# Turning attention probabilities with VectorE and DMA instead of TensorE, with four engine queues in program order

## The chip, the core and the metric

The kernel runs on one core of a Trainium2 chip. The metric is the device time of one execution in microseconds (us). The core's engines are TensorE (PE: matmuls, with its weight loads listed apart as PEld), VectorE (DVE), ScalarE (ACT), GpSimd (POOL) and SyncE (SP, which here only issues DMAs). Each runs its own queue of instructions in order and waits on semaphores for the others.

## What is computed

Two layers over one sequence of 512 tokens of width 1024, in float32: a state-space mixer (layer 0) and a latent attention (layer 1), each behind an RMS norm and added to the residual, then a last RMS norm. The change lies in layer 1:

```python
def mla_mixer(u, positions, in_w, q_norm_w, kv_norm_w, uq_w, ukv_w, out_w):
    proj = u @ in_w                                    # c_q 384, c_kv 256, k_r 64, z 2048
    q = (rms_norm(c_q, q_norm_w) @ uq_w)               # 16 heads of 128 + 64 (rope)
    kv = (rms_norm(c_kv, kv_norm_w) @ ukv_w)           # 16 heads of 128 (keys) + 128 (values)
    ...
    o = causal_block_attention(q_full, k_full, v, MLA_QK_DIM ** -0.5)
    o = o.reshape(bsz, seq, MLA_WIDTH) * jax.nn.silu(z)
    return o @ out_w

# causal_block_attention, for each block of 128 queries:
    s = jnp.where(key_pos[None, :] <= q_pos[:, None], s, -jnp.inf)
    p = jax.nn.softmax(s, axis=-1)
    return jnp.einsum('bhqk,bkhd->bqhd', p.astype(v.dtype), v)
```

## The kernel before

Every float32 matrix product is made of three passes of fp32r matmuls: each operand is split into a high part (a cast, by ACT) and the rest (a subtraction, by DVE), and high x high, high x rest and rest x high are summed in PSUM. So each weight and each activation costs ACT a cast and DVE a subtraction. Weights come as units of 512 KB or less from DRAM into a raw tile (2 buffers, `load_weight`, L260), and `split_weight` (L266) makes whi and wlo (3 buffers each). `prefetch` (L252) loads and splits ahead of use in the order of the list `self.wq`: it splits one weight ahead (`LOOK = 1`) and loads one further.

PE's instructions stand in program order (`tc.manual_schedule` for PE). The other engines' order is chosen by the tile framework's scheduler. `sched` (L237) interleaves two things on PE: a feed, a generator that yields after every few matmuls with their cost, and pieces, functions that each have a due time on the feed's clock.

Layer 1 (`mla`, L650) first projects the input, writes the turned residual to DRAM (ht to hd: VectorE's 32x32 transposes and DMAs with runs of 128 B, L680 to L685), and then goes over 16 heads. For head h the feed is `front_a` in even heads (one rope product for two heads, then q and k of the next pair's first head, L725), `front_b` in odd heads (q and k of the second head, then both heads' values, L750), up to head 10 one gate product `zgemm` (L706), and from head 11 on steps of the first half of the output projection (`out_tok`, L908; KO steps per head). The pieces are:

- `score(h + 1, b)` (L783), b = 0 to 3, due at SC: the next head's scores for query block b, over n = 128 (b + 1) keys: five matmul passes (three for b = 0), mask and row minimum on DVE (L805), exponential with its sum on ACT (L223), reciprocal and scaling on DVE (L807, L808). The probabilities p are queries x keys.
- `turn(h, kb)` (L813), due at TU: for key block kb, PE transposes the 128x128 blocks of p into a PSUM bank (L817, ten per head), ACT casts them to ph (L821), DVE subtracts to get pl (L822).
- `product(h, kb)` (L825), due at PR: three matmuls with the values va, vb into the bank po; after the last one DVE multiplies by the gate z (L837).

`zsilu` (L715) puts SiLU on four gates at a time at the start of heads 4, 8 and 12; the table of functions that ACT holds changes for it, and back for the next exponential. `rope` (L692) multiplies by cosines and, after four swapping DMAs, by sines: three DVE operations. All DMAs of the attention (weights, swaps, residual) are issued by SP. PSUM has eight banks, which scores, products, turned blocks and fronts share in rotation.

Of the kernel before, what the change touches and what calls it, by code (L numbers as in the profile page):

```python
# [15 lines left out]
P = 128  # L16
# [34 lines left out]
OA = 8  # L51
SQ = 2

# [98 lines left out]
class Net:  # L152
# [8 lines left out]
    def build(self):  # L161
# [18 lines left out]
        self.phase, self.group, self.before, self.head = "", [], [], None  # L180
        self.wq = []
        self.wpos = self.wload = 0
        self.wraws = []
        self.wready = {}
        for g in range(NG):
            for i in range(6):
                self.wq.append(("w", U_IN + 6 * g + i))
# [6 lines left out]
        for h in range(14):  # L194
            j = h // 2 + 1
            self.wq += [("ua", j)] if h % 2 == 0 else [("ub", j), ("uc", j)]
            if h < 11:
                self.wq.append(("w", U_MZ + 5 + h))
            self.wq += [out.pop(0) for _ in range({11: 1, 12: 1, 13: 2}.get(h, 0))]
# [6 lines left out]
        with tc.tile_pool(name="ps_m", bufs=1, space=bass.MemoryType.PSUM, reuse_waits="tile") as ps, \  # L206
                tc.tile_pool(name="mla", bufs=2, reuse_waits="tile") as wk:
            self.ps, self.wk = ps, wk
            self.mla()

    LOOK = 1

    def link(self, ins, others):
        for o in others:
# [3 lines left out]
    def E(self, out, in_, func, **k):  # L218
        if self.phase != "E":
            pre = self.nc.scalar.preload_act_table_set("natural_log_exp_and_others")  # L220
            self.link(pre, self.group)
            self.phase, self.group, self.head = "E", [pre], pre
        i = self.nc.scalar.activation(out, in_, func, **k)  # L223
# [23 lines left out]
    def weight(self, kind, idx):  # L247
        key = (kind, idx)
        self.prefetch(self.wq.index(key) + 1 + self.LOOK)
        return self.wready.pop(key)  # L250

    def prefetch(self, want):  # L252
        while self.wload < min(want + 1, len(self.wq)):
            self.wraws.append(self.load_weight(*self.wq[self.wload]))
            self.wload += 1
        while self.wpos < min(want, len(self.wq)):
            self.wready[self.wq[self.wpos]] = list(self.split_weight(self.wraws.pop(0)))[-1]
            self.wpos += 1

    def load_weight(self, kind, idx):  # L260
        n = {"w": 1024, "ua": 1024, "ub": 640, "uc": 512}[kind]
        raw = self.wraw.tile([P, n], F32, tag="raw", name=self.nm("raw"))
        self.nc.sync.dma_start(raw[:], self.t[kind][idx])
        return raw

    def split_weight(self, raw, cuts=()):  # L266
# [4 lines left out]
        for a, b in zip((0, *cuts), (*cuts, n)):  # L271
            nc.scalar.copy(hi[:, a:b], raw[:, a:b])  # L272
            nc.vector.tensor_tensor(lo[:, a:b], raw[:, a:b], hi[:, a:b].bitcast(F32), op=ALU.subtract)  # L273
# [29 lines left out]
    def run(self, g):  # L303
        for _ in g:
            pass
# [54 lines left out]
    def ssm(self):  # L360
# [45 lines left out]
        for i, w in enumerate(ws):  # L406
            self.wready[self.wq[i]] = next(w)
# [242 lines left out]
    def mla(self):  # L650
        tc, nc, t, wk = self.tc, self.nc, self.t, self.wk
        v = nc.vector
        self.bufs = {"b": 8}
        col = lambda i: self.cols[:, i:i + 1]
# [16 lines left out]
        for i in range(6):  # L671
# [6 lines left out]
            if i >= 2:  # L678
                for k in (2 * i - 4, 2 * i - 3):
                    ht = wk.tile([P, T], F32, tag=("ph", "pl")[k % 2], name=self.nm("ht"))  # L680
# [11 lines left out]
        def rope(raw):  # L692
            sw = wk.tile([P, T], F32, tag="rsw", name=self.nm("rsw"), bufs=1)
            for i in range(4):
                j = i ^ 1
                nc.sync.dma_start(sw[32 * i:32 * i + 32, :], raw[32 * j:32 * j + 32, :])
# [374 lines left out]
```

## Time and profile before

| | |
|---|---|
| Median of 3 runs | 836.78 us (836.75 to 837.99) |
| Profiled execution | 836.13 us, of it span 834.0 us |
| Mean granted clock of TensorE | 0.999 |
| ACT busy | 450.4 us (54%) |
| DMA, mean over the span | 109 GB/s, 90.55 MB |
| DMA packets | 50,856, of them 21,552 under 512 B |

The span goes from the first to the last instruction of one profiled execution; the rest of its time lies around the span. A busy time is the part of the span in which the engine had an instruction under way. Matmuls overlap, so the time of one is best read from the starts of its neighbours. A group row ends with the idle time of the engine just before the group's instructions and with what ended it.

### The profile page before, as it was taken

The page shows a single profiled execution, that of the slowest core. Times are in us where ns is not written, and L with a number is a line of the kernel's source. Part 1 is how long each engine was busy: PE and PEld are TensorE (multiplying, and loading weights), DVE is VectorE, ACT ScalarE, POOL GpSimd, SP SyncE. Part 2 cuts the span into 40 slices and gives each one's busy share as a digit, 9 for nine tenths or more (in the row PEclk, how much of TensorE's full clock was granted, in tenths as well). Part 3 has the DMA queues.
Part 4 walks back from the last instruction along what each step waited for, and adds up shares of the span by engine and source line. Part 5 has one row for each costly group of instructions (what it writes and reads, how often), then busy time and mean ns, then how long its engine had stood idle before and what let it go on. Part 6 is the DMA issues. An engine that isn't in the chain of part 4 may idle for free.

```text
span 834.0 us, 11549 instructions
## 1 busy us (share of the span) xinstructions
PE 819.3 (98%) x4228; PEld 691.8 (83%) x4228; DVE 644.9 (77%) x1234; ACT 450.4 (54%) x794; POOL 0.2 (0%) x4
## 2 busy tenths in 40 slices
PE   7999999999999999999999999999999999999996
PEld 5887888888888888888888888888888888888885
DVE  7999898979787989778566787786767869675544
ACT  7567755545465657434353654556547557554233
POOL 0000000000000000000000000000000000000000
PEclk9999999999999999999999999999999999999999
DMA  6364543423242423333555142222222224331212
GB/s 227 103 191 141 155 147 106 152 99 129 101 139 90 152 76 127 115 121 94 130 130 132 54 130 64 79 72 76 63 64 58 90 78 152 101 97 56 86 66 101
DMA packets 50856, 90.55 MB, mean 109 GB/s; under 512 B 21552, under 2 KB 23088, under 8 KB 50800
## 3 DMA queue, kind: packets, MB, share of 16 engines
q1 hardware_dynamic: 50080, 88.77, 34.0%
q10 hardware_dynamic: 720, 1.05, 0.3%
q8 instruction: 33, 0.54, 0.3%
q14 instruction: 23, 0.19, 0.1%
HBM read 83.12 MB, written 4.33 MB: 105 GB/s over the span
## 4 chain that ended last, share of the span: by engine, by line
PE 92%; DVE 3%; DMA 2%; ACT 1%; SPq 1%; issue 0%; DVEq 0%; ACTq 0%
PE mm L291 55%; PE ot L941 11%; PE s L793 5%; PE mm L300 4%; PE po L835 4%; PE mm L773 3%; PE pt L817 2%; PE yd L138 2%; PE yd L291 1%; PE aux L130 1%; PE aux L105 1%; DMA x<-in_x_dram 1%; PE aux L77 1%; PE aux L89 1%; DMA L<-ac_d 1%; DVE wlo L273 1%
## 5 line engine op out<-in xcount | busy, mean ns | idle before, releaser
L272 ACT CAST whi<-raw 128x1024 fp32r<-128x1024 f32 (+3 forms) x132 | 127.0, 965 | 210.3 <-PE mm L291 172.8
L273 DVE TENSOR_TENSOR wlo<-raw,whi 128x1024 fp32r<-128x1024 f32 (+3 forms) x132 | 146.8, 1115 | 54.6 <-ACT whi L272 54.3
L291 PE MATMUL mm<-ah,whi 128*128 128x512 f32 x384 | 154.0, 401 | 0.0
L291 PE MATMUL mm<-ah,wlo 128*128 128x512 f32 x384 | 150.3, 391 | 0.4 <-DVE wlo L273 0.4
L291 PE MATMUL mm<-al,whi 128*128 128x512 f32 x384 | 149.9, 390 | 0.0
L291 PE MATMUL mm<-vh,whi 128*128 128x512 f32 x224 | 89.4, 399 | 0.8 <-ACT whi L272 0.8
L291 PE MATMUL mm<-vh,wlo 128*128 128x512 f32 x224 | 87.9, 392 | 0.7 <-DVE wlo L273 0.7
L291 PE MATMUL mm<-vl,whi 128*128 128x512 f32 x224 | 87.6, 391 | 0.0
L291 PEld LDWEIGHTS mm<-ah,wlo 128*128 128x128 f32 x384 | 72.1, 188 | 16.1 <-DVE wlo L273 0.8
L291 PEld LDWEIGHTS mm<-ah,whi 128*128 128x128 f32 x384 | 72.2, 188 | 15.3 <-issue 1.4
L291 PEld LDWEIGHTS mm<-al,whi 128*128 128x128 f32 x384 | 72.2, 188 | 14.4 <-DVE al L312 0.3
L941 PE MATMUL ot<-whi,ah 128*128 128x512 f32 (+1 forms) x136 | 52.4, 385 | 0.0
L941 PE MATMUL ot<-whi,al 128*128 128x512 f32 (+1 forms) x136 | 51.5, 379 | 0.0
L941 PE MATMUL ot<-wlo,ah 128*128 128x512 f32 (+1 forms) x136 | 51.4, 378 | 0.0
L291 PEld LDWEIGHTS mm<-vh,wlo 128*128 128x128 f32 x224 | 42.1, 188 | 10.7 <-DVE wlo L273 1.5
L291 PEld LDWEIGHTS mm<-vh,whi 128*128 128x128 f32 x224 | 42.2, 188 | 9.4 <-ACT whi L272 1.1
L223 ACT ACTIVATE p<-p,st 128x128 f32<-128x128 f32 (+1 forms) x64 | 36.1, 564 | 25.3 <-DVE st L805 25.2
L291 PEld LDWEIGHTS mm<-vl,whi 128*128 128x128 f32 x224 | 42.2, 188 | 7.3
L821 ACT CAST ph<-pt 128x512 fp32r<-128x512 f32 (+1 forms) x64 | 26.4, 421 | 33.3 <-PE pt L817 32.8
L291 PE MATMUL mm<-ch,whi 128*128 128x512 f32 x104 | 42.6, 410 | 0.0
L291 PE MATMUL mm<-ch,wlo 128*128 128x512 f32 x104 | 40.9, 393 | 0.0
L291 PE MATMUL mm<-cl,whi 128*128 128x512 f32 x104 | 40.8, 392 | 0.0
(223 smaller groups left out, 1637.7 us busy)
## 6 DMA issues: line engine op xcount, KB each, us to landing
raw<-in_w_dram SPq DMA_DIRECT2D x100, 512.0 KB, 3.3
L<-ac_d SPq DMA_DIRECT2D x32, 256.0 KB, 3.9
E<-ea_d SPq DMA_DIRECT2D x32, 128.0 KB, 3.5
raw<-in_ua_dram SPq DMA_DIRECT2D x8, 512.0 KB, 3.3
raw<-in_ub_dram SPq DMA_DIRECT2D x8, 320.0 KB, 2.8
x<-in_x_dram SPq DMA_DIRECT2D x8, 256.0 KB, 4.4
res<-in_x_dram SPq DMA_DIRECT2D x8, 256.0 KB, 3.1
hd<-ht SPq DMA_DIRECT2D x32, 64.0 KB, 3.5
```

The costliest lines, as they stand in the source:

```text
L138: nc.tensor.matmul(yd[64 * h:64 * h + 64, s], self.xdt[j][:, c, h, :], self.L[2 * j + h][:, s], start=True, stop=True)
L223: i = self.nc.scalar.activation(out, in_, func, **k)
L272: nc.scalar.copy(hi[:, a:b], raw[:, a:b])
L273: nc.vector.tensor_tensor(lo[:, a:b], raw[:, a:b], hi[:, a:b].bitcast(F32), op=ALU.subtract)
L291: self.nc.tensor.matmul(ps, a, b, start=i == 0, stop=i == len(seq) - 1)
L300: self.nc.tensor.matmul(p, seq[i][0], seq[i][1], start=i == 0, stop=i == 3 * ks - 1)
L773: nc.tensor.matmul(ps[:, c2 * 256:(c2 + 1) * 256], a, b, start=i == 0, stop=i == 5)
L793: nc.tensor.matmul(ps[:, :n], x[:, s], y[:, :n], start=k == 0, stop=k == 4)
L817: nc.tensor.transpose(pt[:, (b - kb) * P:(b - kb + 1) * P], probs[h][b][:, kb * P:(kb + 1) * P], self.ident)
L821: nc.scalar.copy(ph[:, :n], pt[:, :n])
L835: nc.tensor.matmul(po[:, kb * P:], x, y, start=kb == 0 and k == 0, stop=kb == NCH - 1 and k == 2)
L941: nc.tensor.matmul(ps[:, a:b], x, y, start=start and i == 0, stop=stop and i == 5)
```

## The change

1. **No transposes on PE.** `score` gets a `finish`: after the reciprocal and the scaling DVE turns the block in 32x32 squares (`v.transpose` into pb, 2 buffers), and SP writes it in four DMAs, in runs of 128 B, into a DRAM matrix pd (two, for even and odd heads), keys x queries. `fetch(h)`, a fifth piece of a head's scores, reads the four key blocks back (pl, in buffers of their own for even and odd heads). `turn` is only the cast pl to ph on ACT and the subtraction pl - ph on DVE, in place.
2. **Four queues in program order.** SP's instructions stand in program order in all of `mla`; in the loop over heads DVE, ACT and POOL do too. Subtractions, exponentials, `finish`, the rope and its casts are put off with `defer`: one to five yields of the feed later, or when their result is needed (`now`, `settle`). Without the loop's `lagging` flag they run at once, as before.
3. **Weights and swaps on POOL's queue** in `mla`, and weights split two ahead in the loop (`look = 2`).
4. **New places**: SF, SC, TU, PR and KO. In the heads the first two splits (0.08, 0.17) lie among the next head's scores (0.0 to 0.28), the others (0.47, 0.57) behind the first two products (0.35, 0.45). Head 0's scores move from beside `zgemm(4)` to beside `front_b(0)`. The values' products are a generator of their own, `front_v`, behind the gate product of odd heads. The silus move to 0.8 of heads 3, 7 and 11, with the table change behind them. The output projection splits two gates ahead (`OA = 2`, before 8), and reads the residual at its third weight.

The core of the diff:

```diff
-SF = (0.02, 0.1, 2.1, 3.1)
-SC = (0.0, 0.16, 0.25, 0.44)
-TU = (0.02, 0.08, 0.38, 0.55)
-PR = (0.3, 0.48, 0.65, 0.94)
-KO = (3, 4, 5, 8, 10)
+SF = (0.6, 1.0, 2.0, 3.2, 8.0)
+SC = (0.0, 0.1, 0.18, 0.28, 0.55)
+TU = (0.08, 0.17, 0.47, 0.57)
+PR = (0.35, 0.45, 0.74, 0.94)
+ZS = 0.8
+KO = (4, 4, 4, 8, 10)
-OA = 8
+OA = 2
...
+    def defer(self, fn, lag=1):
+        e = Later(fn, lag)
+        if self.lagging:
+            self.later.append(e)
+        else:
+            e.now()
+        return e
+
+    def tick(self):
+        for e in list(self.later):
+            e.lag -= 1
+            if e.lag <= 0:
+                e.now()
+        self.later = [e for e in self.later if not e.done]
...
         for cost in feed:
             done += cost
+            self.tick()
             while pieces and pieces[0][0] <= done:
                 pieces.pop(0)[1]()
...
-        self.nc.sync.dma_start(raw[:], self.t[kind][idx])
+        self.wqueue.dma_start(raw[:], self.t[kind][idx])
...
+        self.wqueue = nc.gpsimd
...
+            er = self.defer(functools.partial(rope, raw, sw), 3)
+            ea = self.defer(casts, 4)
+            f["w"].append(self.defer(rests, 5))
             yield 1.3
...
-            self.E(p[:], p[:], AF.Exp, scale=-1.0, bias=st[:, 0:1], accum_out=st[:, 1:2])
-            v.reciprocal(st[:, 2:3], st[:, 1:2])
-            v.tensor_scalar(p[:], p[:], st[:, 2:3], None, op0=ALU.mult)
-            probs[h].append(p)
+            p_exp = self.defer(functools.partial(
+                self.E, p[:], p[:], AF.Exp, scale=-1.0, bias=st[:, 0:1], accum_out=st[:, 1:2]))
+
+            def finish():
+                p_exp.now()
+                v.reciprocal(st[:, 2:3], st[:, 1:2])
+                v.tensor_scalar(p[:], p[:], st[:, 2:3], None, op0=ALU.mult)
+                pb = wk.tile([P, T], F32, tag="pb", name=self.nm("pb"))
+                v.transpose(pb[:, :n], p[:])
+                turned = pd[h % 2][:].rearrange("(j a) q -> a j q", a=32)
+                for i in range(4):
+                    q = b * P + 32 * i
+                    nc.sync.dma_start(turned[:, :n // 32, q:q + 32],
+                                      pb[32 * i:32 * i + 32, :n].rearrange("a (j q) -> a j q", q=32))
+
+            ends.append(self.defer(finish, 2))
...
+        def fetch(h):
+            while ends:
+                ends.pop(0).now()
+            for kb in range(NCH):
+                n = T - kb * P
...
+                nc.sync.dma_start(pl.bitcast(F32), pd[h % 2][kb * P:(kb + 1) * P, kb * P:])
+                back[h, kb] = pl
...
         def turn(h, kb):
             n = T - kb * P
-            pt = self.bank("pt")
-            for b in range(kb, NCH):
-                nc.tensor.transpose(pt[:, (b - kb) * P:(b - kb + 1) * P], probs[h][b][:, kb * P:(kb + 1) * P],
-                                    self.ident)
+            pl = back[h, kb]
             ph = wk.tile([P, T], F32R, tag="ph", name=self.nm("ph"))
-            pl = wk.tile([P, T], F32R, tag="pl", name=self.nm("pl"))
-            nc.scalar.copy(ph[:, :n], pt[:, :n])
-            v.tensor_tensor(pl[:, :n], pt[:, :n], ph[:, :n].bitcast(F32), op=ALU.subtract)
-            parts[h].append((ph, pl))
+            nc.scalar.copy(ph[:, :n], pl.bitcast(F32))
+            e = self.defer(functools.partial(
+                v.tensor_tensor, pl, pl.bitcast(F32), ph[:, :n].bitcast(F32), op=ALU.subtract))
+            parts[h].append((ph, pl, e))
...
+        with self.tc.manual_schedule(engines={E.SP, E.DVE, E.Activation, E.Pool}):
+            self.lagging, self.look = True, 2
+            self.sched(chain(front_b(0), front_v(0), zgemm(4)), list(zip(SF, steps(0))))
+            for h in range(MH):
...
+                if h % 2 and h < 14:
+                    feed.append(front_v(j))
                 at = SC if h + 1 < MH else ()
-            pieces = [(x * cost, functools.partial(score, h + 1, b)) for b, x in enumerate(at)]
+                pieces = [(x * cost, fn) for x, fn in zip(at, steps(h + 1))]
...
+                if h < 13 and h % 4 == 3:
+                    pieces.append((ZS * cost, functools.partial(zsilu, h // 4 + 1)))
```

More of the change, by code (lines that the diff above doesn't have):

```diff
@@ L184, in build @@
         self.wready = {}
+        self.later, self.wlater, self.cuts = [], [], {}
         for g in range(NG):
@@ L195, in build @@
             j = h // 2 + 1
[L196 to L199, printed above, removed]
+            self.wq.append(("ub" if h % 2 else "ua", j))
+            self.wq.append(("w", U_MZ + 5 + h) if h < 11 else out.pop(0))
+            if h % 2:
+                self.wq.append(("uc", j))
         self.wq += out
@@ L304, in run @@
         for _ in g:
-            pass
+            self.tick()
     def split(self, src, tagp, pool, n=T, tag=None):
@@ L703, in mla, with settle @@
         zt = []
-        F = [{} for _ in range(8)]
+        F = [{"w": []} for _ in range(8)]
+        def settle(f):
+            for e in f["w"]:
+                e.now()
+            f["w"] = []
         def zgemm(i):
@@ L861, in norm, with steps @@
             return hs, ls
+        def steps(h):
+            return [functools.partial(score, h, b) for b in range(NCH)] + [functools.partial(fetch, h)]
         outg = out0()
```

204 lines of the change are left out of this document (131 added, 73 removed).

## The prediction

> **What bounds the kernel now.** I read the page first (span, busy shares), then the chain that ended last, then what TensorE (PE) waits for.
>
> ```profile
> span 834.0 us, 11549 instructions
> PE 819.3 (98%) x4228; PEld 691.8 (83%) x4228; DVE 644.9 (77%) x1234; ACT 450.4 (54%) x794; POOL 0.2 (0%) x4
> ```
> ```profile
> by line: PE mm L291 55.1%; PE ot L941 10.6%; PE s L793 5.0%; PE mm L300 3.8%; PE po L835 3.6%; PE mm L773 2.7%; PE pt L817 2.1%; PE yd L138 1.8%; PE yd L291 1.3%; PE aux L130 1.3%; PE aux L105 1.1%; DMA x<-in_x_dram 1.0%; PE aux L77 0.7%; P
> ```
> ```profile
> PE mm L300 <- ACT whi L272: 4.8, 1, 4.8
> PE mm L291 <- DVE wlo L273: 1.0, 3, 0.5
> ```
>
> PE is busy for 98% of the span, the chain runs through PE nearly everywhere, and the two longest entries of what PE waited for are 4.8 and 1.0 us in the whole run. So the bound is PE. The line that the change deletes, pt at L817, stands on that chain with 2.1%, which is 17.5 us of 834.0.
>
> Two neighbouring heads of the attention (an even one with front_a, an odd one with front_b) look like this in the table of windows, whose columns are length, then PE, PEld, DVE, ACT and POOL busy:
>
> ```profile
> 541.92:558.95 17.03, 17.03 (x91) 14.56 (x90) 13.34 (x33) 8.55 (x20) 0.00 (x0) 1.00 0.24 76
> 558.95:576.76 17.81, 17.81 (x106) 15.79 (x105) 11.87 (x30) 13.44 (x25) 0.00 (x0) 1.00 0.15 43
> ```
>
> PE is full at a granted clock of 1.00. DVE is the next engine: 13.34 of 17.03 us in the first stretch, 25.2 of 34.84 over both. Before, DVE's order was the scheduler's; that spare time is what the change spends.
>
> **The term that goes: the transposes on PE.** Per head ten 128x128 transposes, in groups of seven, two and one:
>
> ```profile
> 545.99 0.39 PE L817 MATMUL pt<-ident,p 128*128 128x128 f32 x2
> 546.13 0.48 PE L291 MATMUL mm<-vh,whi 128*128 128x512 f32 x1
> 546.45 0.40 PE L291 MATMUL mm<-vl,whi 128*128 128x512 f32 x1
> ...
> 555.93 0.93 PE L817 MATMUL pt<-ident,p 128*128 128x128 f32 x7
> 556.62 0.48 PE L291 MATMUL mm<-ch,whi 128*128 128x512 f32 x1
> 556.93 0.40 PE L291 MATMUL mm<-cl,whi 128*128 128x512 f32 x1
> 557.17 0.40 PE L291 MATMUL mm<-ch,wlo 128*128 128x512 f32 x1
> ...
> 567.10 0.27 PE L817 MATMUL pt<-ident,p 128*128 128x128 f32 x1
> 567.13 0.48 PE L291 MATMUL mm<-vh,whi 128*128 128x512 f32 x1
> 567.44 0.39 PE L291 MATMUL mm<-vl,whi 128*128 128x512 f32 x1
> ```
> ```profile
> L817 PE MATMUL pt<-ident,p 128*128 128x128 f32 x160 | 25.3, 273 | 0.0
> ```
>
> Matmuls are pipelined, so I read starts, not durations. Seven take 0.69 us to the next start, and the matmul after them holds PE for 0.31 where its neighbour takes 0.24: 0.76. Two take 0.14 and delay the next by 0.09: 0.23. One takes 0.03 and delays by 0.08: 0.11. That is 1.10 us a head and 17.6 us over 16 heads, which agrees with the chain's 17.5. The 25.3 us of the grouped row counts overlapping durations and isn't used. PE does everything else as before, only in a somewhat other order, so without new waits the gain is 17.6 us.
>
> **What comes in its place.** DVE turns each head's four score blocks in 32x32 squares (v.transpose), SP writes them to DRAM in 16 DMAs with runs of 128 B, and reads them back in 4. The kernel does the same thing already, to the residual (ht, hd):
>
> ```profile
> L684 SPq DMA_DIRECT2D hd<-ht x32: 341/487/856, 389.0 to 448.9; - x32
> L681 DVE STREAM_TRANSPOSE ht<-res x8: 699/711/712, 388.2 to 431.6; 128x512 f32<-128x512 f32 x8
> ...
> DMA to landing us min/median/max: 2.3/3.5/3.7
> ```
> ```profile
> raw<-in_w_dram SPq DMA_DIRECT2D x100, 512.0 KB, 3.3
> ...
> hr<-hd SPq DMA_DIRECT2D x8, 256.0 KB, 2.9
> ```
> ```profile
> q1 hardware_dynamic: 18642, 8.47, 54.6%
> ```
> ```profile
> q1 hardware_dynamic: 798, 2.02, 19.0%
> ```
>
> The first q1 row is of 388 to 452 us, where the residual is written, the second of 541.92 to 576.76. In the second, 2.02 MB took 19.0% of 16 engines for 34.84 us, 106 engine-us, or 52 per MB. The first holds 16,384 small runs (32 writes of 64 KB in runs of 128 B, 2.1 MB) and 6.37 MB of the rest: 559 engine-us less 331 leaves 228, or 14 ns a run. A head writes 1,280 columns by 128 rows, 5,120 runs: 72 engine-us, 4.5 us on 16 engines. Reading 0.66 MB back costs 34, or 2.1 us; the other traffic is 3.3 us per head. Together 9.9 of some 16.3 us: the engines carry it, so transfers cost latency and not throughput. The writes' issue, 16 at 0.49 us, is 7.8 us of SP a head. SP has nothing else there, because the weight loads move to POOL's queue and with them the four swaps of each rope.
>
> DVE gets the transposes. The trace has one size, 128x512 at 0.71 us; for the smaller ones I take the subtractions of equal size:
>
> ```profile
> L273 DVE TENSOR_TENSOR wlo<-raw,whi 128x1024 fp32r<-128x1024 f32 x3 | 3.7, 1221 | 1.4 <-ACT whi L272 1.4
> ...
> L807 DVE RECIPROCAL st<-st 128x1 f32<-128x1 f32 x8 | 1.3, 160 | 1.0 <-ACT p L223 1.0
> ...
> L822 DVE TENSOR_TENSOR pl<-pt,ph 128x384 fp32r<-128x384 f32 x2 | 1.1, 549 | 0.0
> L808 DVE TENSOR_SCALAR p<-p,st 128x512 f32<-128x512 f32 x2 | 1.0, 484 | 0.0
> ...
> L822 DVE TENSOR_TENSOR pl<-pt,ph 128x256 fp32r<-128x256 f32 x2 | 0.8, 418 | 0.0
> ...
> L822 DVE TENSOR_TENSOR pl<-pt,ph 128x128 fp32r<-128x128 f32 x2 | 0.6, 279 | 0.0
> ```
>
> 0.71 + 0.55 + 0.42 + 0.28 = 1.96 us a head, and nothing leaves DVE (the split of the turned block reads SBUF instead of PSUM at the same size). A pair then asks 25.2 + 3.9 = 29.1 of 34.84 - 2.2 = 32.6 us: DVE is at 89%, and in the even head alone at 13.34 + 1.96 = 15.3 of 17.03 - 1.1 = 15.9. It is not the bound on average, but its queue now runs strictly in program order, so the question is who waits behind what. ACT, with 22.0 of 34.84, is no candidate by its sum.
>
> **The place where program order bites: an even head's third product.** There the rope (three operations, L697 to L699 of before, now deferred by three steps) stands in DVE's queue directly ahead of the third split (128x256) that the third product needs.
>
> ```profile
> 546.54 0.69 DVE L697 TENSOR_TENSOR rraw<-rraw,con 128x512 f32<-128x512 f32 x1
> 547.14 0.69 DVE L698 TENSOR_TENSOR rsw<-rsw,con 128x512 f32<-128x512 f32 x1
> ```
> ```profile
> L223 ACT ACTIVATION_READ_ACCUMULATOR p<-p,st 128x1 f32 x8 | 1.5, 188 | 0.0
> L223 ACT ACTIVATE p<-p,st 128x512 f32<-128x512 f32 x2 | 1.4, 724 | 0.2 <-DVE st L805 0.2
> ...
> L721 ACT CAST k<-mm 128x512 fp32r<-128x512 f32 x2 | 1.2, 580 | 0.0
> ```
> ```profile
> 539.85 2.08 PE mm L291 x9
> ```
>
> A matmul of 512 columns takes 2.08/9 = 0.231 us. From the head's start PE does the 24 matmuls of front_a (5.54) and the next head's scores (five passes over 256, 384 and 512 columns are 11.25 such units, the first block 1.25: 2.89 us): the k product ends at 8.43. First product 0.69, six matmuls 1.39, second product 0.52, twelve matmuls 2.77, two 256-column matmuls of the third product 0.23: at 14.03 PE wants the split. DVE: ACT casts k (0.58, to 9.01) and takes the exponential of the fourth score (0.72 + 0.19, to 9.92). DVE then has reciprocal 0.16, scale 0.48, transpose 0.71, to 11.27; the weight rest 1.22, to 12.49; the rope at a pitch of 0.60, 1.80, to 14.29; the split 0.42, to 14.71. PE is held 0.7 us. Seven even heads (0 to 12) have a front_a: 4.9 us. From below it is nothing (DVE would have to be 0.7 us faster, and the operations overlap by some 0.07 each); below nothing is excluded, since a wait of PE can't be negative. From above it is 1.9 us a head (third rival). An odd head has no rope there and two 64-partition subtractions fewer; the same walk leaves it some 0.8 us to spare, and I cost it at nothing.
>
> **Start and end.** Head 0 has no earlier head to lie beside: its scores move ahead, to six matmuls (1.39 us) after its k product, where k's cast and split (0.58 + 0.69) just fit, and its turned blocks make a whole round trip. Bounds 0 and 3 us (one landing); I take 1.5. The silus go from the start of heads 4, 8 and 12 to the end of the heads before, among ACT work with room: nothing. The cuts of z (two ahead instead of eight) and the later residual reads have four output steps, over 5 us, before they are needed: nothing. The tail after the last matmul is not touched.
>
> **The sum.** 834.0 - 17.6 + 4.9 + 1.5 = 822.8 us of span. The profiled execution took 836.13, so 2.13 lies around the span: 824.9; it was 0.65 below the median of the runs (836.78), so **825.6 us**. The other parts move work between queues and cost nothing as long as the 0.8 us of the odd heads last.
>
> **Rivals.** *First: PE stays full.* DVE's overlaps make up the 0.7 us and only 0.5 is lost at the start: 816.9 of span, 819.7. For it: the before trace shows DVE at 28.4 us of 33.5 without any PE wait:
>
> ```profile
> 681.26:714.74 33.48, 33.48 (x187) 29.17 (x187) 28.41 (x68) 25.44 (x51) 0.00 (x0) 1.00 0.39 120
> ```
>
> Against it: that was in the scheduler's order.
>
> *Second: the change as walked*, 825.6.
>
> *Third: the round trip is late in even heads.* In an odd head (17.81 - 1.1 = 16.7 us) PE ends the fourth score at 7.8 by the same counting, but DVE, which leaves the even head about 2 us late, reduces it by 9.9; exponential 0.91 and finish 1.35 end at 12.2, 4.5 before the head's end. The last write goes out 1.5 us later (3 x 0.49) and lands 2.3 to 3.5 after that, the read 2.9 later: 2.2 to 3.4 us into the even head, while the cast of its first split stands in ACT's queue from 1.4 on (six matmuls), with the next scores' exponentials behind it. Of that wait of 0.8 to 2.0 us DVE's spare 0.6 (15.9 less 15.3) absorbs a part; 0.2 to 1.4 reach PE on top of the 0.7. At 1.9 a head: 13.3 us, 831.2 of span, 834.0. Against it: at the shortest landing it all but vanishes.
>
> *Fourth, on the other side: weights come late from POOL.* No row of before shows a DMA issued there, so its price is unknown. A load goes out one weight ahead of its cast; the one for the even head's first cast is issued at the odd head's last weight (uc), some 3 us earlier, and needs 3.3. Every us that POOL's issue adds holds ACT's cast, then DVE's rest of that weight at the head's first step, and so the whole even head. It turns the result around once it adds some 1.7 us beyond the 0.7 (7 x 2.3 = 16.1). If the issue doubles the landing (3.3 more): 7 x 4.0 = 28, 834.0 - 17.6 + 28 + 1.5 = 845.9, 848.7 in the runs' measure. A gain below nothing from POOL (loads earlier, since SP's queue no longer holds them) would help nobody: PE doesn't wait for loads now.
>
> [...]
>
> *Fifth: gain and new waits cancel*, within 0.2%, when the third's wait and a part of the fourth's come together.
>
> **Chances.** First 0.30, second 0.37, third 0.15, fourth 0.12, fifth 0.06. Why the second: the walk uses rows for all but one size, and the first needs every small delay to fall the right way. Faster by over 0.2% (1.7 us, about what a measurement of this kernel can tell from no change): the first three, 0.82; same 0.06; slower 0.12. The range leaves out the fourth and what lies beyond the bounds: 818 (the first rival less 1.7) to 837 (into the fifth).
>
> **What would show it.** Right: no pt rows; L291's waits in the attention stage short, and the pair of heads near 33.3 us; PE's longest new wait is the po product's on DVE's pl, seven times some 0.7 us; DVE near 88% there. The first: no such wait, a pair at 32.6. The third: ph on ACT waits for DMA in even heads. The fourth: whi on ACT waits for raw, and raw's time to landing, at 3.3 now, is 5 or more. Wrong altogether: an order of PE in which the heads' period does not fall below 34.8.

## The result, and the profile after

The changed kernel takes 877.55 us (median of 4 runs, 874.64 to 880.34) against 836.78: the ratio is 1.0483, 95% interval 1.044 to 1.0527. The forecast was 825.6, with a range to 837. The profiled execution took 880.34 us.

The page of the kernel after, its span, busy row and the row of the granted clock in 40 slices (tenths):

```profile
span 878.3 us, 11881 instructions
PE 823.3 (94%) x4068; PEld 688.0 (78%) x4068; DVE 674.9 (77%) x1298; ACT 449.5 (51%) x794; POOL 50.5 (6%) x100
...
PEclk9999999999999999999999998998999999998998
```

The 160 transposes are gone (4228 matmuls to 4068), yet PE is busy for 4.0 us more than before, and idle for 55.0 (878.3 - 823.3) instead of 14.7. The slices with an 8 are new: before, all of them were 9.

What PE waited for, from 440 us on (us in total, times, longest):

```profile
PE po L941 <- DVE pl L63: 24.3, 10, 4.6
PE po L941 <- ACT ph L924: 9.2, 3, 5.0
PE s L871 <- DVE vb L63: 2.9, 1, 2.9
PE s L874 <- DVE k L63: 0.8, 1, 0.8
PE mm L332 <- DVE wlo L63: 0.7, 1, 0.7
```

The first row is the wait that the prediction named: po on DVE's pl. Seven of its ten are the third products of the even heads 0 to 12, of 4.62, 2.02, 4.11, 3.04, 3.83, 2.27 and 2.56 us, 22.45 together, where the prediction had 7 x 0.7 = 4.9. The second row is head 0 (1.2) and heads 14 and 15 (5.0 and 3.0), whose first products wait for the turned data themselves. Head 14's wait, the longest of all, has a cause of its own in SP's queue:

```profile
770.96 3.95 SPq L1101 DMA_DIRECT2D hr<-hd  x8
775.00 7.72 SPq L896 DMA_DIRECT2D pd<-pb  x8
```

The eight reads of the residual stand between the second and the third block's writes of head 14, and the eight writes behind them land 3.9 to 6.1 us after their issue, where the medians are 1.8 (48 KB) and 2.0 (64 KB).

The table of windows around two of these waits (length, then PE, PEld, DVE, ACT, POOL busy, granted clock, DMA share, GB/s):

```profile
562.00:564.00 2.00, 0.04 (x1) 0.00 (x0) 1.97 (x5) 0.29 (x1) 0.54 (x1) 1.00 0.71 120
564.00:569.00 5.00, 4.93 (x27) 4.32 (x28) 3.24 (x7) 1.56 (x3) 0.00 (x0) 1.00 0.54 164
597.00:600.00 3.00, 0.14 (x2) 0.00 (x0) 2.96 (x5) 0.00 (x0) 0.54 (x1) 1.00 0.58 100
601.00:606.00 5.00, 4.75 (x13) 3.97 (x14) 1.91 (x5) 1.75 (x3) 0.00 (x0) 0.50 0.51 157
```

Each first row is a gap: PE has nothing, DVE is full (1.97 of 2.00, 2.96 of 3.00). After the 2.02 us gap the clock stays at 1.00 and PE does 27 matmuls in 5 us; after the 4.11 us gap it is 0.50 and PE does 13. The trace's record of the clock has nine such spells in the attention stage, of 3.4 or 6.8 us, 41.0 together. PE is busy in 35.4 of them (the rest lies inside the gaps), so about 17.7 us are lost to the half clock. That is most of why PE is busier with less to do: 819.3 - 17.6 + 21.6 = 823.3. The other 3.9 of the 21.6 stay open; the last matmul ahead of a gap counts as busy for some 0.39 us instead of the 0.23 to its neighbour's start, which for 17 gaps is an estimated 2.7 us of it.

So the 44.3 us of span are: 17.6 less for the transposes, 37.9 more in the five rows of waits, 21.6 more for the same matmuls, of it 17.7 at half clock, and 2.4 of idle time in other places, of it 1.6 behind the last matmul (8.8 us of tail against 7.2 before).

The weight loads, whose landing the prediction asked about, and the two new transfers (queue, KB each, median us to landing):

```profile
raw<-in_w_dram SPq DMA_DIRECT2D x64, 512.0 KB, 3.3
raw<-in_w_dram POOLq DMA_DIRECT2D x36, 512.0 KB, 3.7
...
pd<-pb SPq DMA_DIRECT2D x64, 64.0 KB, 2.0
pl<-pd SPq DMA_DIRECT2D x16, 256.0 KB, 2.7
```

Issued by POOL a weight lands in 3.7 us instead of 3.3. The fourth rival said that 5 or more would show it.

### The profile page after: what moved, and what is told of

The parts are those of the page before. It is cut to its first block, busy times and chain, and to the rows that moved or that the text cites. A ratio compares the mean times of both kernels' runs of the same rounds, so it can differ in the third digit from the quotient of the medians.

```text
span 878.3 us, 11881 instructions
## 1 busy us (share of the span) xinstructions
PE 823.3 (94%) x4068; PEld 688.0 (78%) x4068; DVE 674.9 (77%) x1298; ACT 449.5 (51%) x794; POOL 50.5 (6%) x100
## 4 chain that ended last, share of the span: by engine, by line
PE 62%; DVE 16%; DMA 11%; SPq 4%; ACT 4%; issue 3%; DVEq 0%; POOL 0%; ACTq 0%
PE mm L332 41%; PE ot L1055 6%; DMA pd<-pb 5%; PE mm L341 4%; SPq L896 3%; DMA pl<-pd 3%; DVE wlo L63 2%; PE yd L149 2%; PE po L941 2%; DVE pb L892 1%; DVE p L890 1%; PE yd L332 1%; PE aux L141 1%; PE s L871 1%; PE aux L116 1%
## 5 line engine op out<-in xcount | busy, mean ns | idle before, releaser
L332 PE MATMUL mm<-vh,wlo 128*128 128x512 f32 x224 | 89.8, 401 | 1.2 <-DVE wlo L63 1.2
L303 POOL DMA_DIRECT2D raw<-in_w_dram x36 | 19.2, 534 | 629.9 <-DMA hd<-ht 417.7
L924 ACT CAST ph<-pl 128x512 fp32r<-128x512 f32 (+1 forms) x64 | 27.8, 454 | 52.9 <-DMA pl<-pd 42.4
L63 DVE TENSOR_TENSOR pl<-pl,ph 128x512 fp32r<-128x512 f32 (+1 forms) x64 | 30.0, 481 | 25.7 <-ACT ph L924 25.7
L941 PE MATMUL po<-pl,va 128*128 128x512 f32 (+1 forms) x64 | 23.9, 374 | 24.3 <-DVE pl L63 24.3
```

The source lines that it names most:

```text
L63: self.fn()
L303: self.wqueue.dma_start(raw[:], self.t[kind][idx])
L332: self.nc.tensor.matmul(ps, a, b, start=i == 0, stop=i == len(seq) - 1)
L924: nc.scalar.copy(ph[:, :n], pl.bitcast(F32))
L941: nc.tensor.matmul(po[:, kb * P:], x, y, start=kb == 0 and k == 0, stop=kb == NCH - 1 and k == 2)
```

## The experiments

**The theories.** A: DVE comes late to the even heads' third split because of what stands ahead of it in its queue (the weight rest, the rope), and each gap then costs a second time by the half clock. B, its rival: the round trip over DRAM is too long, in whatever order the queues stand. C, which some expectations name, is the fourth rival: weights come late from POOL. One more, D, was formed after the first eight runs and is told there. Times are medians in us; ratios are to the kernel before on the same chip, with their 95% interval.

**e1_split3_early.** The third split ahead of the weight rest and the rope.

```diff
-TU = (0.08, 0.17, 0.47, 0.57)
+TU = (0.08, 0.17, 0.40, 0.57)
```

> Edit: only TU's third entry, 0.47 to 0.40. In even heads this puts one instruction, the third split (128x256) on DVE, ahead of the weight rest and the rope instead of behind them; PE's order stays. Theory A (DVE's order makes the wait in the seven even heads, and the granted clock falls to half after each): about 22 us of waiting and 14 us of half clock go, 842 to 848 us, and the rows of PE waiting for pl before the 128x256 product vanish. Theory B (the round trip through DRAM is the bound, the wait only shows at this product): the wait moves to the first product and the time stays above 865. Theory C (weights from POOL are late): unchanged, 875 to 880.

864.27 (two runs, 860.61 and 867.93), ratio 1.0328 (1.0224 to 1.0432): 13.3 us gained, less than half of the 30 to 36 that A expected. PE's idle time between 440 and 870 us fell from 38.1 to 27.4, but the waits on pl did not go: they spread over 15 products.

**e2_fill.** Ten idle matmuls of 512 columns into a spare bank ahead of each even head's third product, so that PE works where it waited.

```diff
+            if kb == 2 and h % 2 == 0 and h < 14:
+                fill = self.bank("fill")
+                for k in range(10):
+                    nc.tensor.matmul(fill[:], va[:, :P], va[:], start=True, stop=True)
```

> Edit: ten matmuls of 512 columns (2.3 us) into a bank that nobody reads, ahead of the third product of heads 0, 2, ... 12. They add work and take no wait away. Theory A: they lie inside the wait that is there anyway and keep PE from idling, so the half-clock spells behind these products go or shorten; 862 to 870 us, faster although PE does 70 more matmuls. If the half clock costs nothing of its own, or is not caused by the waits: 878 or more, up to 16 us slower where a wait was shorter than the filling.

871.01 (869.99 to 872.02), ratio 1.0408 (1.0378 to 1.0438): with 70 matmuls more, some 16 us of PE work at 0.231 each, the kernel is 6.5 us faster. The granted clock went from 0.974 to 0.988, and the half-clock spells of the stage from 41.0 us to 17.1. That the half clock costs by itself is shown.

**e3_weights_sp.** Weights back on SP's queue.

```diff
-        self.wqueue = nc.gpsimd
+        self.wqueue = nc.sync
```

> Edit: layer 1's weight loads are issued by SP as before the change; the rope's swaps stay on POOL. Theory C (POOL's issue makes weights late): 10 us or more faster. Theory A and B: no gain; SP now has weight loads between the writes of the turned blocks, in program order, and a load that waits for its raw buffer holds up the writes behind it: the same or slower, 875 to 890.

916.34, ratio 1.095 (1.0918 to 1.0981). What ACT waited for in this kernel, from 440 us on:

```profile
ACT whi L312 <- DMA raw<-in_w_dram: 32.3, 9, 12.5
ACT whi L312 <- DMA raw<-in_ub_dram: 27.6, 7, 6.9
```

In program order SP's weight loads stand behind writes that wait for DVE. With SP in program order POOL's queue is what keeps the weights early, so C falls. What SP would do in the order of before is not tried here.

**e4_pe_turn.** The transposes back on PE, everything else of the change kept (program order, places, POOL's queue).

```diff
-                v.transpose(pb[:, :n], p[:])
...
+            for b in range(kb, NCH):
+                nc.tensor.transpose(pt[:, (b - kb) * P:(b - kb + 1) * P], probs[h][b][:, kb * P:(kb + 1) * P],
+                                    self.ident)
```

> Edit: PE's transposes are back (turn as before the change), DVE's transposes, the writes and the reads are gone; the four queues in program order, the places and the weights on POOL stay. Theory A: the third split is still behind the weight rest and the rope, but DVE has 2 us a head less to do; some of the wait stays: 838 to 850 us. Theory B: without the round trip nothing is late: 834 to 838, as before the change. Theory C: still slow, above 860.

849.61, ratio 1.0152 (1.0123 to 1.0182). What PE waited for here, from 440 us on:

```profile
PE pt L908 <- DVE vb L63: 2.9, 1, 2.9
PE po L929 <- DVE pl L63: 2.9, 3, 1.2
```

So program order, the new places and the rest of the change cost 12.8 us with no round trip at all. The long waits at the products belong to the round trip or to DVE's transposes, which e4 takes out together: 849.6 - 17.6 would be 832.0, and it is 877.6.

**e5_sched_order.** The turn by DVE and DMA, with the queues in the scheduler's order, nothing deferred, weights one ahead.

```diff
-        with self.tc.manual_schedule(engines={E.SP, E.DVE, E.Activation, E.Pool}):
-            self.lagging, self.look = True, 2
+        if True:
+            self.lagging, self.look = False, 1
```

> Edit: the turn by DVE and DMA, the places and the weights on POOL stay, but SP, DVE, ACT and POOL take the scheduler's order again, nothing is put off, and weights are split one ahead. If program order is what costs (theory A in its wider form: an instruction that waits holds those behind it): below 850 us. If the round trip and DVE's added work cost in any order (theory B): 865 or more. Before the runs so far: program order with PE's transposes cost 12.8 us over the kernel before, so program order alone explains less than a third of the 41 us.

881.44, ratio 1.0535 (1.0477 to 1.0592). What PE waited for, its longest row:

```profile
PE po L940 <- ACT ph L923: 35.1, 15, 5.2
```

The waits moved to the first products, as many us as before. At this point B looked right.

**e6_no_rope.** The rope's three DVE operations of heads 2 to 15 are left out, which is a part of the computation; DVE has 2 us less to do in each even head.

```diff
+            if not self.lagging:
...
+                v.tensor_tensor(raw[:], raw[:], sw[:], op=ALU.add)
```

> Edit to the changed kernel: the rope's three DVE operations are left out for heads 2 to 15 (so that part of the computation is missing); swaps and casts stay. This takes 1.8 us off DVE in each even head, at the place where the split waits. Theory A as a matter of DVE's load (its queue is near full in even heads, any 1.8 us would do): the seven waits shrink to under 0.5 us each and their half-clock spells go, 838 to 846 us, more than the 13 us that moving the split alone gave. Theory B: the waits move to the first product, above 860.

870.42, ratio 1.0403 (1.032 to 1.0486). What PE waited for, its first two rows:

```profile
PE po L942 <- DVE pl L63: 23.9, 18, 2.7
PE po L942 <- ACT ph L925: 8.8, 4, 6.8
```

24.3 us of waits on pl became 23.9, now in even and odd heads alike. The first split's casts of heads 1 and 13 in this run are

```profile
531.13 0.62 ACT L925 CAST ph<-pl 128x512 fp32r<-128x512 f32 x1 [4.87 <-DMA pl<-pd]
...
759.60 0.62 ACT L925 CAST ph<-pl 128x512 fp32r<-128x512 f32 x1 [3.94 <-DMA pl<-pd]
```

so a head takes 19.0 us on the average, as in the changed kernel (19.1, below), although DVE has less to do. DVE's load is not the cause: A falls, but for the half clock, of which this run has 20.5 us of spells instead of 41.0.

**e7_silu_early** (e1 with ZS = 0.6) and **e8_rope_pool** (e7 with the rope's two multiplications on GpSimd).

> Edit to e1 (third split early): the silus of heads 3, 7 and 11 at 0.6 instead of 0.8, behind the fourth split's cast instead of between the two casts of the values. In e1 the second cast and DVE behind it stand still for 4.7 us there. If that hold is what the following even head pays for: the waits of heads 4, 8 and 12 go and the wait of a score for vb's bank (2.9 us) too, 8 to 12 us below e1's 864. If the waits come from DVE's load alone: no change, 860 to 866.

> Edit to e7: the rope's two multiplications go from DVE to GpSimd, which was idle apart from issuing DMAs. Theory A by load: 1.2 us a head pair off DVE, the remaining waits of even heads shrink by about that, 5 to 9 us below e7. [...]

858.84, ratio 1.0265 (1.0235 to 1.0294), and 857.38, ratio 1.0247 (1.0218 to 1.0277): 5.4 us for the silus' place, 1.5 for the rope. Both are less than expected, and with two runs each, and 7 us between those of e1, the first isn't clear of noise.

**Theory D: a ring.** The trace of the changed kernel over one head, an even head 2 (start, duration, engine, line, operation; in brackets the idle time before it and its releaser):

```profile
543.14 0.71 DVE L892 STREAM_TRANSPOSE pb<-p 128x512 f32<-128x512 f32 x1 [0.86 <-DMA pd<-pb]
547.36 1.76 SPq L917 DMA_DIRECT2D pl<-pd  x4
551.30 0.62 ACT L924 CAST ph<-pl 128x512 fp32r<-128x512 f32 x1 [2.40 <-DMA pl<-pd]
552.31 0.40 ACT L257 ACTIVATE p<-p,st 128x128 f32<-128x128 f32 x1
...
553.70 9.03 SPq L896 DMA_DIRECT2D pd<-pb  x16
...
557.64 0.19 ACT L257 ACTIVATION_READ_ACCUMULATOR p<-p,st 128x1 f32 x1
...
558.15 0.58 DVE L892 STREAM_TRANSPOSE pb<-p 128x384 f32<-128x384 f32 x1 [0.90 <-DMA pd<-pb]
...
559.23 0.14 DVE L889 RECIPROCAL st<-st 128x1 f32<-128x1 f32 x1
...
559.93 0.71 DVE L892 STREAM_TRANSPOSE pb<-p 128x512 f32<-128x512 f32 x1
...
566.71 1.76 SPq L917 DMA_DIRECT2D pl<-pd  x4
...
569.49 0.62 ACT L924 CAST ph<-pl 128x512 fp32r<-128x512 f32 x1 [3.23 <-DMA pl<-pd]
```

Read it as a loop. The cast at 551.30 waits for head 2's turned data. Head 3's first exponential (552.31) stands behind it in ACT's queue, and with it head 3's scalings and transposes on DVE, the last of which ends at 560.64: 9.34 us. In these lies a wait of 0.90: pb has two buffers, so the third block's transpose waits until the first block's writes have landed, and those are late by the cast. The fourth block's exponential ends at 557.83 and DVE reaches its reciprocal at 559.23, 1.40 later; the third product, which the prediction held for 0.7 us with DVE on time, waits 2.02. Then the last of 16 writes goes out (562.73), it lands and the reads start (566.71), and their data reach head 3's own first cast at 569.49: 2.1 + 4.0 + 2.8 = 8.85 us. 9.34 + 8.85 = 18.19 us from cast to cast; PE needs half of the prediction's 34.84 - 2.2 for a head, 16.3. Over twelve heads (532.21 to 761.32) these casts come 19.1 us apart: the first part takes 9.2 to 12.6 us from head to head, the second 7.5 to 9.9. The loop is not rigid, for in e1, which moves the third split alone, the same casts come 17.9 us apart (531.40 to 746.67); why was not followed. Each head hands its lateness on to the next one's turning, so slack in one head doesn't make it good. The rope isn't in the ring, which fits e6's unchanged 19.0 us. D's remedy is a place: the first two splits behind the next head's exponentials instead of ahead of them.

**e9_splits_late** and **e10_late_hr** (e9 with ZS = 0.7 and the residual's reads halved and one step later).

```diff
-TU = (0.08, 0.17, 0.47, 0.57)
-PR = (0.35, 0.45, 0.74, 0.94)
+TU = (0.28, 0.40, 0.52, 0.65)
+PR = (0.50, 0.62, 0.90, 0.94)
```

> Edit: the changed kernel with other places alone, TU = (0.28, 0.40, 0.52, 0.65) and PR = (0.50, 0.62, 0.90, 0.94): the first two splits of a head stand behind the next head's first exponentials instead of ahead of them, and its first products follow later. Theory D (a ring: the first split of a head waits for its turned data on ACT and DVE, and the next head's exponentials, scalings and transposes stand behind it in those queues, so one round trip of some 8.9 us and DVE's chain of some 9.3 us behind it add up to more than a head's 16.3 us on PE): with the splits behind that chain the round trip lies beside it, the heads come down to 16.5 to 18 us, PE's idle time between 440 and 870 falls from 38 to under 18, half-clock spells to three or fewer, 825 to 845 us in all. Theory A (DVE's load or rope ahead of the third split) and theory B (the round trip bounds in any order): the waits stay, now at the first products, idle above 30, 860 or more.

> Edit: the late places of the run beside it, the silus at 0.7 instead of 0.8, and the reads of the residual in halves of 512 columns, issued one output step later. Theory D: as the run beside it, less what the silus hold of DVE's vb in heads 3, 7 and 11 (three times 1 to 2 us with the half clock behind it): 3 to 6 us below that run. If the residual's reads stand ahead of the round trips of the last heads on SP's queue, heads 14 and 15 wait less: 1 to 4 us more. Theory B: within 3 us of that run.

e9: 859.01 (854.51 to 859.47), ratio 1.0266 (1.0249 to 1.0283), 18.5 us less than the change; e10: 854.82, ratio 1.021 (1.0195 to 1.0225). Who waited for the transfers of pd, in the change and then in e9, from the view of that tile:

```profile
  ACT ph L924: 42.4, 10
  DVE pb L892: 7.3, 9
```
```profile
  DVE pb L892: 13.1, 13
  ACT ph L924: 2.8, 2
```

The ring is open: ACT's casts wait 2.8 us for the data instead of 42.4. PE's idle time fell from 38.1 to 21.0 us, the half-clock spells of the stage from nine to three (the profiled execution is the fastest of the six, 854.51). The products moved too, by up to 0.17 of a head, so e9 alone doesn't tell a ring from a round trip that was merely too close to its product. e6 speaks for the ring: a product that is merely too early would have gained from the 2 us that DVE is spared, and the heads came no closer. But D had promised under 18 us and 825 to 845. What is left shows in the same view: DVE itself waits 13.1 us in 13 places for pb. And in e9's trace ACT's two table loads (1.28 us each) and four silus (2.2) still keep DVE idle for 4.5 us three times.

**e11_sched_late** and **e12_sched_later**: e5 with e9's places, and with later ones.

```diff
-TU = (0.08, 0.17, 0.47, 0.57)
-PR = (0.35, 0.45, 0.74, 0.94)
+TU = (0.42, 0.52, 0.64, 0.74)
+PR = (0.66, 0.76, 0.90, 0.96)
```

> Edit: the turn by DVE and DMA in the scheduler's order of the queues, nothing deferred, weights one ahead (the run e5_sched_order, 881.4 us), with TU = (0.28, 0.40, 0.52, 0.65) and PR = (0.50, 0.62, 0.90, 0.94). In e5 PE waited at the first product of 15 heads, 35 us in all, 2.3 a head and up to 5.2, with some 20 us of half clock behind it. Theory D (the wait is the distance from a head's last exponential to its first product being shorter than the round trip and the chain behind it): the first product is 0.15 of a head later, 2.5 us, and so the waits of 2 us and less go, of the longer ones 0.5 to 2.7 stay; idle 10 to 20 us between 440 and 870, 835 to 852 us. Theory B (the round trip's ring bounds in any order and at any place): the waits move to the new places, 870 or more.

> Edit: as the run beside it, with TU = (0.42, 0.52, 0.64, 0.74) and PR = (0.66, 0.76, 0.90, 0.96): the first product 0.31 of a head, 5 us, later than in e5_sched_order. Theory D: all waits of e5 but those near 5 us go, idle under 12, 825 to 842 us, unless the next head's own turning is then held behind the splits (waits at the products of the head after, 845 to 855). Theory B: 870 or more.

867.94, ratio 1.0359 (1.0335 to 1.0384), and 867.8, ratio 1.0355 (1.0336 to 1.0374): a third of e5's loss goes, and 5 us more of distance do no more than 2.5. Both theories miss. In e11 ACT waited only 7.1 us for the landing of pl, but 64.4 for DVE's reductions, and at 554 us, in the rows read, the casts stood right behind the last exponential; so a place in the program doesn't fix where the scheduler puts the cast. Why it puts it there was not tried.

**e13_silu_even, e14_all, e15_all_pool.** e13 is e9 with the later silus in the middle of heads 4, 8 and 12, behind the third split's cast. e14 is e10 with that, and four buffers for pb. e15 is e14 with the rope's multiplications on GpSimd.

```diff
-                if h < 13 and h % 4 == 3:
-                    pieces.append((ZS * cost, functools.partial(zsilu, h // 4 + 1)))
+                if h and h % 4 == 0:
+                    pieces.append((ZS * cost, functools.partial(zsilu, h // 4)))
...
-                pb = wk.tile([P, T], F32, tag="pb", name=self.nm("pb"))
+                pool, g, m = (self.nrm, "sq", SQ) if b % 2 else (wk, "pb", 2)
+                pb = pool.tile([P, T], F32, tag=g, name=self.nm("pb"), bufs=m)
```

> Edit: e9_splits_late with the three later groups of silus moved from the end of heads 3, 7 and 11 to the middle of heads 4, 8 and 12, behind the third split's cast and ahead of the fourth's. In e9 ACT's two table loads and four silus stand between two casts of va and keep DVE idle for some 4.5 us three times. Theory D with that hold as what is left: DVE has the rope and the weight rest to do meanwhile, the hold falls to some 1 us, the waits at the first two products of heads 4, 8 and 12 and the 2.9 us at the scores of head 12 go, 5 to 9 us of idle and 2 to 4 of half clock less: 843 to 850 us. If DVE's load as such is what is left: within 3 us of e9.

> Edit: e10_late_hr with the silus as in e13_silu_even, and four buffers for pb instead of two (two of them from a tag that the odd heads' fourth block gives up by sharing a tile). In e9 DVE waited 13.1 us in 13 places for pb's writes to land. Theory D: this and the residual's halves give 3 to 8 us beyond e13: 836 to 846 us. If DVE's load as such is what is left: no lower than e13 by more than 2 us.

> Edit: e14_all with two of the rope's three operations on GpSimd, from head 2 on. If DVE's load is what is left, 1.4 us of DVE less in seven even heads make this 3 to 8 us faster than e14_all; if it isn't, within 2 us of it, as e8_rope_pool was of e7_silu_early (1.5).

e13: 850.2, ratio 1.0166 (1.0149 to 1.0182). e14: 836.23, ratio 0.9989 (0.998 to 0.9999). e15: 839.0, ratio 1.0026 (1.0015 to 1.0037). The silus' hold was worth 8.8 us; the buffers of pb and the residual's reads together 14.0. In e10 these reads and the silus at 0.7 were worth 4.2 together, so most of the 14.0 should be the buffers', which no run shows by itself. What PE waited for in e13 and then in e14, the first row of each:

```profile
PE po L941 <- DVE pl L63: 12.4, 12, 2.5
```
```profile
PE po L945 <- DVE pl L63: 5.2, 5, 1.5
```

DVE's row of waits for pb's writes (15.2 us in e13) is not in e14's list any more. With the rope's multiplications on GpSimd e14 gets 2.8 us slower, so less load on DVE doesn't help; whether GpSimd's operations cost something of their own was not separated.

**e16_last_heads** (e14 with PR = (0.62, 0.72, 0.92, 0.96) from head 11 on, and head 0's scores 0.2 to 0.3 of the feed's clock later) and **e17_tail** (e16 with the second half of the output projection outside program order).

```diff
+PL = (0.62, 0.72, 0.92, 0.96)
...
+                pieces += [(x * cost, functools.partial(product, h, b)) for b, x in enumerate(PL if h > 10 else PR)]
```

> Edit: e14_all with PR = (0.62, 0.72, 0.92, 0.96) from head 11 on and SF = (0.9, 1.3, 2.3, 3.4, 8.0) for head 0's scores. Theory D, where a product's place is what makes PE wait: the waits of 1.5, 0.9 and 1.5 us at the first products of heads 11, 13 and 14 and the 0.8 us at head 0's first score go, with the 3.4 us half-clock spell behind head 12's staying: 2 to 5 us below e14_all, 831 to 834. If DVE's load sets the floor in those heads: the waits move to later products, within 1 us of e14_all.

> Edit: e16_last_heads with the second half of the output projection outside the program order, in the scheduler's order and nothing deferred. The tail after PE's last matmul is 9.1 us in e14_all and 7.5 before: if program order makes it longer, 1 to 2 us below e16_last_heads; else within 0.5.

e16: 833.9 (12 runs), ratio 0.9968 (0.9957 to 0.998). e17: 832.69, ratio 0.9947 (0.9935 to 0.996): this version beats the kernel before by 0.5%. Its page, and what PE waited for from 440 us on:

```profile
span 830.8 us, 11920 instructions
PE 807.8 (97%) x4068; PEld 676.8 (81%) x4068; DVE 674.3 (81%) x1298; ACT 448.8 (54%) x794; POOL 50.5 (6%) x100
```
```profile
PE po L946 <- DVE pl L64: 3.8, 5, 1.3
PE po L946 <- ACT ph L929: 2.2, 3, 0.8
PE s L875 <- DVE k L64: 0.8, 1, 0.8
PE mm L333 <- DVE wlo L64: 0.7, 1, 0.7
```

DVE is as busy as in the changed kernel (674.3 against 674.9 us); PE has 7.5 us of waits instead of 37.9, and of the half clock one spell of 3.4 us is left. The last two rows, at head 0, are those of the changed kernel to a tenth; the 0.8 us at the first score stayed, so that part of e16's edit did nothing.

## Why the prediction was wrong, point by point

- **The transposes, -17.6 us: right as far as it can be read.** They are gone, but the full 17.6 shows in no run. 819.3 - 17.6 + 17.7 of half clock is 819.4 us of PE, against 823.3 measured; e17 with its one spell (1.7) should come to 803.4 and has 807.8. The 4 us or so that are too many each time are the open part of the sum above.
- **DVE's transposes, 1.96 us a head: right.** By size, in the groups of the changed kernel (mean ns behind the busy time), they take 2.05 us a head:

```profile
L892 DVE STREAM_TRANSPOSE pb<-p 128x512 f32<-128x512 f32 x16 | 11.4, 712 | 2.9 <-DMA pd<-pb 2.4
L892 DVE STREAM_TRANSPOSE pb<-p 128x384 f32<-128x384 f32 x16 | 9.3, 578 | 5.2 <-DMA pd<-pb 4.9
L892 DVE STREAM_TRANSPOSE pb<-p 128x256 f32<-128x256 f32 x16 | 7.1, 446 | 0.6
...
L892 DVE STREAM_TRANSPOSE pb<-p 128x128 f32<-128x128 f32 x16 | 5.0, 312 | 0.8 <-DVE p L890 0.3
```

- **The place of the loss: right. Its size: wrong, and this is the step that failed.** The even heads' third product waits on pl, as walked. But the walk started every even head with DVE on time and let the round trip be a latency: "the engines carry it, so transfers cost latency and not throughput". The third rival had the pieces (the cast of the first split in ACT's queue "with the next scores' exponentials behind it", a round trip of 6.7 to 7.9 us by its terms, where the trace has 7.45 and 8.85), and its sign came true, with 42.4 us of ACT's casts waiting for the data. But it charged them once per even head, 0.2 to 1.4 us. It didn't follow the lateness on into the next head and back: a latency inside a loop that goes round once a head is a throughput, here 18.2 us against 16.3. e6, where a head still takes 19.0 us with the rope gone, and e9, which opens the loop with places alone and gains 18.5 us, show it. So the term of 7 x 0.7 = 4.9 us measured 22.45; in head 2 the 1.3 us beyond the 0.7 are DVE's lateness (1.40 us at the fourth reciprocal, where the walk had none).
- **Odd heads at nothing: right as a price.** PE waited 0.3 us at the products of the odd heads 1 to 13. But the 0.8 us to spare was counted from a DVE on time, and the ring runs through the odd heads too: in e6, with the rope gone, the waits stand in odd heads as well.
- **pb's two buffers: overlooked.** They are in the diff, and DVE waits 7.3 us for them in the change, inside the ring, and 13.1 in e9. e14, which lifts them along with the silus' and the residual's places, comes to 836.2.
- **The later residual reads at nothing: wrong.** The prediction priced their use alone. On SP's queue they stand ahead of head 14's last eight writes, and its first product waits 5.0 us with 6.8 us of half clock behind.
- **"The other parts move work between queues and cost nothing": wrong.** Program order, places and POOL's queue cost 12.8 us with PE's transposes (e4). Of that the silus between two casts of va are one part: the 2.9 us in e4's first row is the bank that vb holds there, and the wait for vb is gone in e13. The tail after the last matmul, "not touched" in the prediction, is another, 1.6 us longer, and 7.4 us again in e17.
- **The granted clock: left out of the sum.** A PE wait was priced at its own length. The half clock made the 37.9 us of waits cost about half as much again (17.7).
- **The fourth rival, weights late from POOL: refuted**, by 3.7 us to landing, and because its sign is missing: from 440 us on no cast of ACT waits for a weight's load. In program order SP's queue would be 38.8 us worse (e3). Where the 0.4 us beyond SP's median of 3.3 come from no run shows.
- **The start, +1.5: low.** The gaps up to head 0's second product are 0.71, 0.82, 1.19 and 0.62 us, 3.3 together.
- **Not settled:** what the remaining part of e4's 12.8 us is, where 4 us of PE's busy time go, and why the scheduler's order keeps waits at any place (e11, e12). e14's gain is that of several edits together: the buffers were not tried alone.

## What to carry to other kernels

When a change puts a round trip between a step and its next turn, look for the loop before pricing the latency: follow the queue position of the first instruction that waits for the data, and ask whether the next turn's work stands behind it. If it does, add up the loop and compare it with the bound engine's period; the remedy is to place the waiting instruction behind the next turn's work, and to give the source tile as many buffers as there are writes in flight. Look too at what else stands in the queue that issues the round trip. Where the bound engine's clock is at half behind its waits, as PE's was here (37.9 us of waits and an estimated 17.7 us lost at half clock), price a wait of a few us at more than its length.

## What the runs showed of the hardware

**The clock behind PE's gaps.** In the changed kernel a spell at half clock followed every PE gap of 2.27 us or more (2.27, 2.56, 2.94, 2.99, 3.04, 3.83, 4.11, 4.62, 5.02), starting inside the gap or at most 1.3 us behind it, and lasted 3.4 us in six cases and 6.8 in three; the gap of 2.02 us had none. In e14 two gaps of 1.17 and 0.63 us, which ended at 724.75 and 725.77, brought a spell of 3.4 us as well. PE's timeline in e14, two matmuls ahead of these gaps and two behind them:

```profile
715.27 0.39 PE L332 MATMUL mm<-cl,whi 128*128 128x512 f32 x1
715.50 0.39 PE L332 MATMUL mm<-ch,wlo 128*128 128x512 f32 x1
...
727.43 0.63 PE L332 MATMUL mm<-ch,wlo 128*128 128x512 f32 x1
727.85 0.63 PE L332 MATMUL mm<-ch,whi 128*128 128x512 f32 x1
```

Starts are 0.23 us apart ahead, 0.42 behind. But in e9 a gap of 2.96 us (771.05 to 774.01) brought none, nor did one of 2.94 in e2 (735.17 to 738.11, with starts 0.23 us apart behind it), so in these traces the length of a gap alone doesn't decide; what does is left open. Windows around the gap in e9:

```profile
771.00:774.00 3.00, 0.05 (x1) 0.00 (x0) 1.20 (x3) 1.33 (x2) 0.00 (x0) 1.00 0.31 52
774.00:784.00 10.00, 9.85 (x46) 8.04 (x47) 6.33 (x12) 3.59 (x7) 0.53 (x1) 1.00 0.70 178
```

**A round trip over DRAM** of a head's probabilities (16 writes in runs of 128 B, four reads) took 7.45 and 8.85 us from the end of the last transpose to the cast that reads them, in the rows shown. The medians to landing are 2.0 and 2.7 us, but the reads wait for the last of 16 writes, which landed 4.2 us after its issue in the second case, and issue comes on top (1.76 us for the four reads).
